# A hybrid decoder layer: head factors brought to the channels by a transpose, a small store and a broadcast load

## The chip, the cores and the metric

The kernel runs on one core of a Trainium2 chip. A core has a matrix engine (PE), a vector engine (DVE), an activation engine (ACT), a general engine (POOL) and an engine that issues transfers (SP); each works through its own queue in order, and they wait for each other on semaphores. The metric is the time of one execution on the device in microseconds (us), lower is better. Whole executions are timed several times; one more is run under the profiler, and its trace is what the readings below come from.

## The reference

One layer over 1024 tokens of 1024 channels, all in float32. Three branches read one projection of the normalized input. The parts that the change touches, cut to what matters:

```python
# RWKV-7 branch, 8 heads of 64 channels
kk = split_heads(k * k_k, 8, 64)
kk = kk / jnp.maximum(jnp.sqrt(jnp.sum(kk * kk, -1, keepdims=True)), 1e-12)
a = jax.nn.sigmoid(a0 + al @ a2)
# recurrence per token, with b = kk * a:
#   S = S * w + (S @ -kk) b^T + v k^T ;  y = S r
# stick-breaking attention, 8 heads of 64; cross attention, 4 heads of 128
k = rms_norm(split_heads(k, heads, hd), k_g)
```

In each of the three the channels of a key are divided by one number per token and head: the root of the sum of squares over the head's channels. Those numbers are the head factors.

## The kernel before

Data lies with channels on the 128 partitions and 1024 tokens along the free axis, so one tile holds two heads of 64 channels (or one of 128). A sum over channels is a sum over partitions, done on PE: `head_ss` (L267) takes 128 tokens of the squares at a time as the stationary operand and multiplies them by the two columns of `ind`, so the sums come out with tokens on partitions, 16 columns (8 groups of tokens by 2 heads). The power −0.5 runs on POOL on that small tile. To multiply the channels by the factors they must lie along the free axis again and on all channels of a head. Before the change, `expand_heads` (L249) copies each factor to 64 columns on DVE, a 128 x 1024 tile `ex`, and `bcast_heads` (L258) transposes it on PE in eight pieces of 128x128 into two PSUM banks. The product with the channels then reads PSUM.

This is done in nine places:

- `rwkv_prep` (L302), four times (p = 0 to 3), about 58 us apart from 55 us on: Sigmoids after low-rank products (L315, L316), a square of k (L320), a scan on DVE (L327), `head_ss` (L330), the power (L334), a second low-rank product (L338), exponentials (L340 to L343), `ex` (L344), transposes of v, and then the product (L366) and `b` (L367). `chain` (L376 to L379) builds operands from them on DVE, `gram` multiplies them on PE and masks the result on DVE (L393), `turned` transposes `bp` (L405).
- `sb_qk` (L746), four times, from 300 to 550 us: `k_fin` copies and squares a projection, `k_ss` makes `ex`, `k_bc` (L766) multiplies, `k_split` (L775 to L778) splits the keys for two-pass matmuls.
- `mem_kss` and `mem_kbc` (L965, L984), once, near 680 us, for the 256 memory tokens and 4 heads of 128.

How the work is ordered: functions are generators. Projections are items of eight steps; a step is six matmuls (`mm3`: two halves of three products of high and low parts). `stream` runs the items in a list, and `weave` runs one step of them for each `yield` of a main function (`rwkv_prep`, then the attention). A hook, given to an item as `{k: function}`, is called after step k. `need(name)` runs items until a named result exists. In most of the kernel the matmuls and transposes (L112, L105) are pinned: PE executes them in the order in which the program writes them. The other engines' orders are not pinned. A planner lays them out when the program is built, by its own costs and by priority (`rwkv_prep` has a higher one than the items), and each engine then keeps that order. Each weight tile is loaded by SP (L76) into one of two buffers, copied in its high part by ACT (L80), and split by POOL (L81), which frees the buffer.

Tiles come from pools with a fixed number of buffers per tag: `w4` has 3, `qk` 8, `it` 1, the PSUM tags `mm` and `g` 4 banks each.

Of the kernel before, what the change touches and what calls it, by code (L numbers as in the profile page):

```python
# [26 lines left out]
SBD = 64  # L27
# [22 lines left out]
class Trunk:  # L50
# [67 lines left out]
    def setup(self):  # L118
        nc, tc = self.nc, self.tc
        E = self.ctx.enter_context  # L120
        self.pool_c = E(tc.tile_pool(name="const", bufs=1))
        self.bufs_p = {"mm": 4, "g": 4}
        self.pool_ps = E(tc.tile_pool(name="psum", bufs=4, space=bass.MemoryType.PSUM))
        self.pool_d = E(tc.tile_pool(name="dram", bufs=1, space=bass.MemoryType.DRAM))
        self.pool_wt = E(tc.tile_pool(name="weights", bufs=2))
        self.pool_s = E(tc.tile_pool(name="small", bufs=2))
        self.kon = self.pool_c.tile([128, NKON], F32, name="kon")
        self.params = self.pool_c.tile([128, NPAR], F32, name="params")
        nc.sync.dma_start(self.params, self.I["params"])

        def kon(n):
            o, w = KON[n]
            return self.kon[:, o : o + w]

        self.ident, self.blk, self.ones = kon("ident"), kon("blk"), kon("ones")
        self.mm_mask, self.ind = kon("mm"), kon("ind")
        self.scr = self.pool_d.tile([4, NG, 128, 1024], F32, name="scr")
        self.mad = self.pool_d.tile([128, 64, 64], F32, name="mad")
        self.vd = self.pool_d.tile([2, 2, NG, 64, 4, 64], F32, name="vd")
        self.td = self.pool_d.tile([2, NG, 2, 64, 2, 128], F32, name="td")  # L140
        self.yd = self.pool_d.tile([3, 4, 128, 1024], F32, name="yd")
        self.mrd = self.pool_d.tile([8, 128, 1024], F32, name="mrd")
        self.gsd = self.pool_d.tile([3, 8, 128, 1024], F32, name="gsd")
        self.x2d = self.pool_d.tile([8, 128, 1024], F32, name="x2d")
        self.vmd = self.pool_d.tile([128, 1024], F32, name="vmd")
        self.vsd = self.pool_d.tile([T + 1, 512], F32, name="vsd")
        self.actd = self.pool_d.tile([NF // 2, 7, 128, 512], F32, name="actd")
        self.ggd = self.pool_d.tile([4, 2, 128, 1024], F32, name="ggd")

    def consts(self):  # L150
        nc = self.nc
# [94 lines left out]
        nc.vector.scalar_tensor_tensor(out, pr, self.omm[:, ti : ti + 1], tmp, ALU.mult, ALU.add)  # L246
        return out

    def expand_heads(self, f, tag="w4"):  # L249
        nc = self.nc  # L250
        ex = self.t4(tag)
        nc.vector.tensor_copy(
            ex[:, :1024].rearrange("p (j h i) -> p j h i", j=8, h=2),
            f.rearrange("p (j h) -> p j h", j=8).unsqueeze(3).to_broadcast([128, 8, 2, 64]),
        )
        return ex

    def bcast_heads(self, ex):  # L258
        out = []
# [42 lines left out]
    def rwkv_prep(self, p, krv, need):  # L302
        nc = self.nc
        lora, wa = self.lora, self.wa
        cs = slice(p * 128, (p + 1) * 128)
        halves = [slice(0, 512), slice(512, 1024)]
# [2 lines left out]
                yield  # L309
        need(f"k{p}")  # L310
        k = krv[0]
        a, su = self.t4("qk"), self.t4("qk")
        for hs in halves:
            pa, pu = self.ps("g"), self.ps("g")
            self.mmul(pa, lora[64:128, cs], wa[64:128, hs], start=True, stop=True)  # L315
            self.mmul(pu, lora[0:64, cs], wa[0:64, hs], start=True, stop=True)  # L316
            nc.scalar.activation(a[:, hs], pa, AF.Sigmoid, bias=self.par("a0", p))
            nc.scalar.activation(su[:, hs], pu, AF.Sigmoid, bias=self.par("w0", p))
        P = self.t4("qk")
        nc.scalar.activation(P, k, AF.Square, scale=self.par("k_k", p))  # L320
        kp = self.t4("qk")
        nc.scalar.activation(kp, a, AF.Identity, scale=self.par("k_a", p), bias=self.omka[:, p : p + 1])
        nc.vector.tensor_tensor(kp, k, kp, ALU.mult)
# [1 line left out]
            yield  # L325
        cc = Q = su
        nc.vector.tensor_tensor_scan(cc, self.seg, su, 0.0, ALU.mult, ALU.add)  # L327
        for _ in range(2):
            yield
        pst = self.head_ss(P)  # L330
        mx = self.small("rs", [128, 16])
        nc.vector.tensor_scalar(mx, pst, 1e-24, None, ALU.max)
        inv = self.small("inv", [128, 16])
        nc.gpsimd.tensor_tensor(inv, mx, self.half[:, :16], ALU.pow)  # L334
        g = self.t4("qk")
        for hs in halves:
            pgh = self.ps("g")
# [3 lines left out]
        pc = self.pc[p]  # L341
        nc.scalar.activation(pc, cc.rearrange("p (c s) -> p c s", c=NC)[:, :, 63], AF.Exp, scale=-EXPM)
        nc.scalar.activation(Q, cc, AF.Exp, scale=EXPM, bias=self.offs[:, 1:2])  # L343
        ex = self.expand_heads(inv, "it")  # L344
        for _ in range(3):
            yield
        need(f"v{p}")
        r, v = krv[1], krv[2]
# [13 lines left out]
        for _ in range(2):  # L362
            yield
        kk, b = k, a
        for hs, bc in zip(halves, self.bcast_heads(ex)):
            nc.vector.scalar_tensor_tensor(kk[:, hs], k[:, hs], self.par("k_k", p), bc, ALU.mult, ALU.mult)  # L366
        nc.vector.tensor_tensor(b, kk, a, ALU.mult)  # L367

        def chain(h):
            hs = halves[h]  # L370
# [298 lines left out]
                self.mmul(pt[e * 64 : e * 64 + 64, u * 4 : u * 4 + 4], vl8[0:8, u * 64 : u * 64 + 64], self.ident[0:8, e:8:2], start=True, stop=True)  # L669
        nc.vector.tensor_copy(self.vlast, pt[:, :32])  # L670

    def head_norm(self, pst, nh, width, fold, neg=None):
        nc = self.nc
        n = 8 * nh
        t = self.small("hn", [128, 16])
        v3 = lambda x: x[:, :n].rearrange("p (j h) -> p j h", j=8)
        b3 = lambda x: x.unsqueeze(2).to_broadcast([128, 8, nh])
        nc.vector.tensor_tensor(v3(t), v3(pst), b3(self.rsc2), ALU.mult)
        f = self.small("hf", [128, 16], bufs=4)
        self.rsqrt(f[:, :n], t[:, :n], n, 1.0 / (width * fold * fold), 1e-6 / (fold * fold))  # L680
        if neg is not None:
            nc.gpsimd.tensor_tensor(v3(neg), v3(f), b3(self.rscn), ALU.mult)
            return neg
        nc.gpsimd.tensor_tensor(v3(f), v3(f), b3(self.rsc), ALU.mult)
        return f

    def proj_item(self, src, fin, hook={}):
# [58 lines left out]
    def sb_qk(self, p, out):  # L746
        nc = self.nc
# [8 lines left out]
            st["k"] = sq, kr  # L756

        def k_ss():
            st["ex"] = self.expand_heads(self.head_norm(self.head_ss(st["k"][0]), 2, SBD, 1.0))

        def k_bc():
            kr = st["k"][1]
            bc = self.bcast_heads(st["ex"])
            for h in range(2):
                hs = slice(h * 512, (h + 1) * 512)
                nc.vector.scalar_tensor_tensor(kr[:, hs], kr[:, hs], self.par("sbk"), bc[h], ALU.mult, ALU.mult)  # L766
            st["K"] = [], []

        def k_split(i):
# [31 lines left out]

        w = self.I["w_in"]
        hooks = {1: lambda: k_split(1), 3: q_ss, 4: lambda: q_split(0), 6: lambda: q_split(1)}
        kq = {4: k_bc, 5: lambda: k_split(0)}
        return self.proj_item(w[18 + p], k_fin), k_ss, self.proj_item(w[14 + p], q_fin, kq), hooks

    def sb_attn(self, qk, need):
# [157 lines left out]
    def mem_kss(self):  # L965
        nc = self.nc
        sq, kr, rm, rm2 = self.mk
        pst = self.ps("g")
        for h in range(4):
            for j in range(2):  # L970
                i = h * 2 + j
                self.colsum(pst[:, i : i + 1], sq[:, i * 128 : (i + 1) * 128], self.ones[:, 0:1])
        fk = self.small("hf", [128, 16], bufs=4)
        f3 = fk[:, :8].rearrange("p (h j) -> p h j", j=2)
        b3 = lambda x: x.unsqueeze(1).to_broadcast([128, 4, 2])
        t = self.small("hn", [128, 16])
        nc.vector.tensor_tensor(t[:, :8].rearrange("p (h j) -> p h j", j=2), pst[:, :8].rearrange("p (h j) -> p h j", j=2), b3(rm2), ALU.mult)
        self.rsqrt(fk[:, :8], t[:, :8], 8, 1.0 / 128, 1e-6)
        nc.vector.tensor_tensor(f3, f3, b3(rm), ALU.mult)
        ex = self.t4()  # L980
        nc.vector.tensor_copy(ex[:, :1024].rearrange("p (i c) -> p i c", i=8), fk[:, :8].unsqueeze(2).to_broadcast([128, 8, 128]))
        self.mk = kr, ex

    def mem_kbc(self):  # L984
        nc = self.nc
        kr, ex = self.mk
        for i in range(2):
            hs = slice(i * 512, (i + 1) * 512)
            pt = self.ps("g")
            for j in range(4):  # L990
                self.transpose(pt[:, j * 128 : (j + 1) * 128], ex[:, (i * 4 + j) * 128 : (i * 4 + j + 1) * 128])
            nc.vector.tensor_tensor(kr[:, hs], kr[:, hs], pt, ALU.mult)
        self.vm = self.t4("A")
        nc.sync.dma_start(self.vm, self.vmd)
        self.kx = [self.t4("A", F32R), self.t4("A", F32R)]
        nc.scalar.activation(self.kx[0], kr, AF.Copy)
        nc.vector.tensor_tensor(self.kx[1], kr, self.kx[0].bitcast(F32), ALU.subtract)
# [691 lines left out]
    def run(self):  # L1689
# [34 lines left out]
        for h in range(4):  # L1724
            mqi[h] = self.mem_q(h, mq[h], {2: mqi[h - 1][1], 4: mark(f"mq{h - 1}")} if h > 1 else {})
        items += [gate({0: prep}), gate(), gate({2: prep}), mss, *mv, *mk, mqi[0][0], mark("kv")]
        items += [self.mem_kss, gate({1: mqi[0][1]}), self.mem_kbc, mqi[1][0], mark("mq0")]
        items += [mqi[2][0], mqi[3][0], gate({2: mqi[3][1], 4: mark("mq3")}), gate(), mark("mem")]
        ld1, br1 = self.branch(1, True)
        ld2, br2 = self.branch(2, False)  # L1730
# [113 lines left out]
```

## Time and profile before

| | |
|---|---|
| median of 3 runs | 1872.44 us (1870.16 to 1873.26) |
| the profiled execution, whole | 1876.17 us |
| its span, first to last instruction | 1874.4 us |
| mean granted PE clock | 0.988 of full speed |
| ACT, POOL busy | 886.5, 783.2 us |
| moved by DMA | 261.29 MB |

Busy time of an engine is the time in which it executes; a wait is idle time of an engine that ended when another engine or a transfer was done. In a list of instructions in order of time, a row has its start, its length, engine, line, operation, what it writes and reads, how many instructions are merged in it, and in brackets the idle time ahead of it and what ended that. A row of one line's durations has minimum, median and maximum in ns. A row of transfers has the issuing queue, the count, the size of each and the median time from issue to landing.

### The profile page before, as it was taken

The page shows a single profiled execution, that of the slowest core. Times are in us where ns is not written, and L with a number is a line of the kernel's source. Part 1 is how long each engine was busy: PE and PEld are TensorE (multiplying, and loading weights), DVE is VectorE, ACT ScalarE, POOL GpSimd, SP SyncE. Part 2 cuts the span into 40 slices and gives each one's busy share as a digit, 9 for nine tenths or more (in the row PEclk, how much of TensorE's full clock was granted, in tenths as well). Part 3 has the DMA queues.
Part 4 walks back from the last instruction along what each step waited for, and adds up shares of the span by engine and source line. Part 5 has one row for each costly group of instructions (what it writes and reads, how often), then busy time and mean ns, then how long its engine had stood idle before and what let it go on. Part 6 is the DMA issues. An engine that isn't in the chain of part 4 may idle for free. (4 is left out here: it accounts for less than half of the span.)

```text
span 1874.4 us, 27394 instructions
## 1 busy us (share of the span) xinstructions
PE 1801.7 (96%) x10468; PEld 1453.9 (78%) x10468; DVE 1170.8 (62%) x1638; ACT 886.5 (47%) x1665; POOL 783.2 (42%) x448
## 2 busy tenths in 40 slices
PE   8999999999999999998999899979999999999999
PEld 6777778778787887776777688757888888878877
DVE  5657665998887323323333682476777677785586
ACT  5443343556566635534545433454444444554433
POOL 2322342322222442112233431477676767645454
PEclk9999999999999999999999999999999999999999
DMA  4255565211112441566734573222333233386475
GB/s 177 57 172 176 166 214 162 64 48 43 51 54 66 137 109 54 191 204 227 269 126 175 173 235 111 92 88 84 113 107 107 85 124 100 125 311 211 140 240 187
DMA packets 120037, 261.29 MB, mean 139 GB/s; under 512 B 28249, under 2 KB 40793, under 8 KB 119778
## 3 DMA queue, kind: packets, MB, share of 16 engines
q1 hardware_dynamic: 82434, 193.71, 32.1%
q10 hardware_dynamic: 33696, 53.23, 7.8%
q0 software_dynamic: 3776, 12.62, 2.2%
q8 instruction: 82, 1.34, 0.3%
q14 instruction: 49, 0.40, 0.1%
HBM read 178.99 MB, written 80.48 MB: 138 GB/s over the span
## 5 line engine op out<-in xcount | busy, mean ns | idle before, releaser
L81 POOL TENSOR_TENSOR wl<-wr,wh 128x1024 fp32r<-128x1024 f32 x77 | 195.9, 2545 | 507.7 <-ACT wh L80 507.7
L112 PE MATMUL mm<-xhi,wh 128*128 128x512 f32 x784 | 265.2, 419 | 9.1 <-ACT xhi L179 7.4
L112 PE MATMUL mm<-xlo,wh 128*128 128x512 f32 x784 | 246.0, 395 | 0.9 <-DVE xlo L180 0.9
L112 PE MATMUL mm<-xhi,wl 128*128 128x512 f32 x784 | 243.8, 392 | 0.0
L112 PEld LDWEIGHTS mm<-xlo,wh 128*128 128x128 f32 x784 | 149.0, 190 | 34.8 <-DVE xlo L180 1.6
L112 PEld LDWEIGHTS mm<-xhi,wl 128*128 128x128 f32 x784 | 148.3, 189 | 33.5 <-POOL wl L81 0.5
L112 PEld LDWEIGHTS mm<-xhi,wh 128*128 128x128 f32 x784 | 139.0, 192 | 39.8 <-issue 9.1
L80 ACT ACTIVATE wh<-wr 128x1024 fp32r<-128x1024 f32 x77 | 81.4, 1057 | 158.8 <-PE mm L112 86.3
L112 PE MATMUL mm<-dw,da 128*128 128x512 f32 x528 | 121.4, 390 | 1.6 <-DVE da L1584 1.4
L112 PE MATMUL mm<-BT,wh 128*128 128x512 f32 x352 | 110.4, 395 | 7.8 <-DVE u L1397 7.8
L112 PE MATMUL mm<-BT,l 128*128 128x512 f32 x504 | 117.6, 389 | 0.0
L112 PEld LDWEIGHTS mm<-dw,da 128*128 128x128 f32 x528 | 98.8, 188 | 23.6 <-DVE da L1584 2.3
L1585 POOL TENSOR_TENSOR dw<-draw,dw 128x512 fp32r<-128x512 f32 x55 | 80.5, 1471 | 85.9 <-ACT dw L1583 83.1
L831 DVE TENSOR_TENSOR_SCAN at<-at,at 128x128 f32<-128x128 f32 (+3 forms) x64 | 91.2, 1427 | 32.1 <-ACT at L825 32.0
L112 PE MATMUL mm<-B,wh 128*128 128x512 f32 x352 | 108.5, 389 | 2.1 <-ACT p L1439 2.1
L112 PEld LDWEIGHTS mm<-BT,l 128*128 128x128 f32 x504 | 94.6, 188 | 19.6
L1584 DVE TENSOR_TENSOR da<-draw,da 128x512 fp32r<-128x512 f32 x77 | 65.9, 864 | 61.4 <-ACT da L1582 60.8
L112 PE MATMUL g<-dw,da 128*128 128x512 f32 x396 | 92.4, 394 | 3.0 <-ACT dw L1583 1.9
L733 DVE TENSOR_TENSOR w<-w,rbc 128x1024 f32<-128x1024 f32 x24 | 49.2, 2048 | 68.4 <-ACT w L732 68.3
L1345 POOL TENSOR_TENSOR l<-it,l 128x1024 fp32r<-128x1024 f32 x21 | 50.8, 2420 | 97.9 <-ACT l L1344 97.9
L112 PEld LDWEIGHTS g<-dw,da 128*128 128x128 f32 x396 | 75.5, 191 | 19.5 <-ACT dw L1583 2.3
L1582 ACT ACTIVATE da<-draw 128x512 fp32r<-128x512 f32 x77 | 48.3, 628 | 85.1 <-PE mm L112 40.8
(322 smaller groups left out, 4002.4 us busy)
## 6 DMA issues: line engine op xcount, KB each, us to landing
wr<-in_w_in_dram SPq DMA_DIRECT2D x50, 512.0 KB, 3.6
draw<-actd SPq DMA_DIRECT2D x77, 256.0 KB, 3.8
at<-scr SPq DMA_DIRECT2D x32, 512.0 KB, 5.4
draw<-in_w_down_dram SPq DMA_DIRECT2D x55, 256.0 KB, 4.9
wr<-in_w_up_dram SPq DMA_DIRECT2D x22, 512.0 KB, 3.6
actd<-gall ACTq DMA_DIRECT2D x44, 256.0 KB, 3.2
rw<-in_w_up_dram SPq DMA_DIRECT2D x20, 512.0 KB, 3.8
gsd<-w ACTq DMA_DIRECT2D x18, 512.0 KB, 2.7
```

The costliest lines, as they stand in the source:

```text
L80: self.nc.scalar.activation(hi, raw, AF.Copy)
L81: self.nc.gpsimd.tensor_tensor(lo, raw, hi.bitcast(F32), ALU.subtract)
L112: self.pinned(self.nc.tensor.matmul(*a, **k))
L733: nc.vector.tensor_tensor(g, g, self.rbc, ALU.mult)
L831: self.pinned(nc.vector.tensor_tensor_scan(sn[:, :W][:, ::-1], sn[:, :W][:, ::-1], self.smask[:, 1024 - W :][:, ::-1], 1.0, ALU.mult, ALU. ...
L1345: nc.gpsimd.tensor_tensor(lo, src, hi.bitcast(F32), ALU.subtract)
L1582: self.pinned(nc.scalar.activation(A[:, 0], a, AF.Copy))
L1584: self.pinned(nc.vector.tensor_tensor(A[:, 1], a, A[:, 0].bitcast(F32), ALU.subtract))
L1585: nc.gpsimd.tensor_tensor(Wt[:, 1], w, Wt[:, 0].bitcast(F32), ALU.subtract)
```

## The change

The nine places get the factors in another way. `factors` allocates `ex`, sets its first 128 columns to zero on POOL and lets POOL or DVE write the 16 (for memory 8) factors straight into its first columns, sorted by head and then by group of tokens. `rows_out` transposes that one block of 128x128 on PE, copies 16 rows of the result back to SBUF on ACT, and stores them (8 KB) to a small DRAM tile `fd` from ACT's queue. `rows_in` loads each head's 4 KB row from there onto all partitions of the head, from SP's queue: two loads of 64 partitions, for memory one of 128. The products read `ex` in SBUF.

In `rwkv_prep` the square and `head_ss` come ahead of the first low-rank products, one step apart from each other, and the power follows at once; `rows_out` comes ahead of the second low-rank product, `rows_in` one step after it, and `b` is made in halves. The number of steps in `rwkv_prep` stays. In `sb_qk`, `rows_out` hangs on step 2 of the Q projection, `rows_in` on step 4, `k_bc` on step 6 and the first `k_split` on step 7; before, they were on steps 4 and 5. For memory `rows_out` hangs on step 3 of a gate projection and `rows_in` on step 5.

```diff
+    def factors(self, tag="w4"):
+        ex = self.t4(tag)
+        self.nc.gpsimd.memset(ex[:, 0:128], 0.0)
+        return ex, ex[:, :16].rearrange("p (h j) -> p j h", j=8)
+
+    def rows_out(self, ex, name, n=16):
+        nc = self.nc
+        pt = self.ps("g")
+        self.transpose(pt[:, :128], ex[:, :128])
+        nc.scalar.activation(ex[0:n, 128:256], pt[0:n, :128], AF.Copy)
+        nc.scalar.dma_start(self.fd[name][0:n], ex[0:n, 128:256])
+
+    def rows_in(self, ex, name, heads=2):
+        w = 128 // heads
+        for h in range(heads):
+            self.nc.sync.dma_start(
+                ex[h * w : (h + 1) * w, :1024],
+                self.fd[name][h * 8 : (h + 1) * 8].rearrange("j p -> (j p)").unsqueeze(0).to_broadcast([w, 1024]))
...
 rwkv_prep:
+        P = self.t4("qk")
+        nc.scalar.activation(P, k, AF.Square, scale=self.par("k_k", p))
+        yield
         a, su = self.t4("qk"), self.t4("qk")
+        pst = self.head_ss(P)
         for hs in halves:
...
+        ex, inv = self.factors("it")
+        mx = self.small("rs", [128, 16])
+        nc.vector.tensor_scalar(mx, pst, 1e-24, None, ALU.max)
+        nc.gpsimd.tensor_tensor(inv, mx.rearrange("p (j h) -> p j h", j=8), self.half[:, :16].rearrange("p (j h) -> p j h", j=8), ALU.pow)
...
         nc.vector.tensor_tensor_scan(cc, self.seg, su, 0.0, ALU.mult, ALU.add)
-        for _ in range(2):
-            yield
-        pst = self.head_ss(P)
...
+        yield
+        self.rows_out(ex, f"r{p}")
         g = self.t4("qk")
...
-        ex = self.expand_heads(inv, "it")
-        for _ in range(3):
+        yield
+        self.rows_in(ex, f"r{p}")
+        for _ in range(2):
             yield
...
-        for hs, bc in zip(halves, self.bcast_heads(ex)):
-            nc.vector.scalar_tensor_tensor(kk[:, hs], k[:, hs], self.par("k_k", p), bc, ALU.mult, ALU.mult)
-        nc.vector.tensor_tensor(b, kk, a, ALU.mult)
+        for hs in halves:
+            nc.vector.scalar_tensor_tensor(kk[:, hs], k[:, hs], self.par("k_k", p), ex[:, hs], ALU.mult, ALU.mult)
+            nc.vector.tensor_tensor(b[:, hs], kk[:, hs], a[:, hs], ALU.mult)
...
 sb_qk:
-            st["ex"] = self.expand_heads(self.head_norm(self.head_ss(st["k"][0]), 2, SBD, 1.0))
+            st["ex"], f = self.factors()
+            self.head_norm(self.head_ss(st["k"][0]), 2, SBD, 1.0, into=f)
...
+            nc.vector.scalar_tensor_tensor(kr, kr, self.par("sbk"), st.pop("ex"), ALU.mult, ALU.mult)
...
-        kq = {4: k_bc, 5: lambda: k_split(0)}
+        kq = {2: lambda: self.rows_out(st["ex"], f"s{p}"), 4: lambda: self.rows_in(st["ex"], f"s{p}"), 6: k_bc, 7: lambda: k_split(0)}
...
 run:
-        items += [self.mem_kss, gate({1: mqi[0][1]}), self.mem_kbc, mqi[1][0], mark("mq0")]
+        items += [self.mem_kss, gate({1: mqi[0][1], 3: lambda: self.rows_out(self.mk[1], "m", 8), 5: lambda: self.rows_in(self.mk[1], "m", 1)}), self.mem_kbc, mqi[1][0], mark("mq0")]
```

More of the change, by code (lines that the diff above doesn't have):

```diff
@@ L148, in setup @@
         self.ggd = self.pool_d.tile([4, 2, 128, 1024], F32, name="ggd")
+        self.fd = {n: self.pool_d.tile([16, 128], F32, name=f"fd{n}") for n in ("r0", "r1", "r2", "r3", "s0", "s1", "s2", "s3", "m")}
     def consts(self):
@@ L247, in shifted @@
         return out
-    def expand_heads(self, f, tag="w4"):
-        nc = self.nc
[L251 to L256, printed above, removed]
+    def factors(self, tag="w4"):
[3 more added lines that the diff above has]
+    def rows_out(self, ex, name, n=16):
+        nc = self.nc
+        pt = self.ps("g")
[8 more added lines that the diff above has]
+                self.fd[name][h * 8 : (h + 1) * 8].rearrange("j p -> (j p)").unsqueeze(0).to_broadcast([w, 1024]))
     def bcast_heads(self, ex):
@@ L318, in rwkv_prep @@
             nc.scalar.activation(su[:, hs], pu, AF.Sigmoid, bias=self.par("w0", p))
-        P = self.t4("qk")
-        nc.scalar.activation(P, k, AF.Square, scale=self.par("k_k", p))
+        ex, inv = self.factors("it")
+        mx = self.small("rs", [128, 16])
+        nc.vector.tensor_scalar(mx, pst, 1e-24, None, ALU.max)
+        nc.gpsimd.tensor_tensor(inv, mx.rearrange("p (j h) -> p j h", j=8), self.half[:, :16].rearrange("p (j h) -> p j h", j=8), ALU.pow)
         kp = self.t4("qk")
@@ L327, in rwkv_prep @@
         nc.vector.tensor_tensor_scan(cc, self.seg, su, 0.0, ALU.mult, ALU.add)
-        for _ in range(2):
-            yield
-        pst = self.head_ss(P)
[L331 to L334, printed above, removed]
+        yield
+        self.rows_out(ex, f"r{p}")
         g = self.t4("qk")
@@ L670, in spread_last, with head_norm @@
         nc.vector.tensor_copy(self.vlast, pt[:, :32])
-    def head_norm(self, pst, nh, width, fold, neg=None):
+    def head_norm(self, pst, nh, width, fold, neg=None, into=None):
         nc = self.nc
@@ L683, in head_norm @@
             return neg
-        nc.gpsimd.tensor_tensor(v3(f), v3(f), b3(self.rsc), ALU.mult)
+        nc.gpsimd.tensor_tensor(v3(f) if into is None else into, v3(f), b3(self.rsc), ALU.mult)
         return f
@@ L758, in k_ss @@
         def k_ss():
-            st["ex"] = self.expand_heads(self.head_norm(self.head_ss(st["k"][0]), 2, SBD, 1.0))
+            st["ex"], f = self.factors()
+            self.head_norm(self.head_ss(st["k"][0]), 2, SBD, 1.0, into=f)
         def k_bc():
             kr = st["k"][1]
[L763 to L766, printed above, removed]
+            nc.vector.scalar_tensor_tensor(kr, kr, self.par("sbk"), st.pop("ex"), ALU.mult, ALU.mult)
             st["K"] = [], []
@@ L978, in mem_kss @@
         self.rsqrt(fk[:, :8], t[:, :8], 8, 1.0 / 128, 1e-6)
-        nc.vector.tensor_tensor(f3, f3, b3(rm), ALU.mult)
-        ex = self.t4()
-        nc.vector.tensor_copy(ex[:, :1024].rearrange("p (i c) -> p i c", i=8), fk[:, :8].unsqueeze(2).to_broadcast([128, 8, 128]))
+        ex, _ = self.factors()
+        nc.vector.tensor_tensor(ex[:, :8].rearrange("p (h j) -> p h j", j=2), f3, b3(rm), ALU.mult)
         self.mk = kr, ex
@@ L986, in mem_kbc @@
         kr, ex = self.mk
[L987 to L992, printed above, removed]
+        nc.vector.tensor_tensor(kr, kr, ex, ALU.mult)
         self.vm = self.t4("A")
```

## The prediction

> **What bounds the kernel now.** I read the page first, then busy time by stretch, then the waits of PE in the stretch where the change acts, then single instructions in order of time.
>
> ```profile
> span 1874.4 us, 27394 instructions
> PE 1801.7 (96%) x10468; PEld 1453.9 (78%) x10468; DVE 1170.8 (62%) x1638; ACT 886.5 (47%) x1665; POOL 783.2 (42%) x448
> ...
> 39.90:300.00 260.10, 250.36 (x1386) 192.70 (x1385) 159.80 (x190) 107.69 (x131) 86.14 (x39) 0.99 0.51 161
> 300.00:700.00 400.00, 391.40 (x2681) 321.73 (x2680) 290.16 (x282) 221.81 (x398) 124.78 (x64) 1.00 0.24 72
> ...
> PE g L105 <- DVE at L393: 6.4, 3, 2.5
> PE g L112 <- DVE qk L379: 2.4, 2, 1.8
> ```
>
> The first two lines are the whole kernel, the next two the stretches that hold the four `rwkv_prep` (40 to 300) and the `sb_qk` and memory work (300 to 700): length, then busy us of PE, PEld, DVE, ACT, POOL. PE is idle 9.7 us of 260 and 8.6 us of 400. So the kernel is PE in a fixed order, and a microsecond of PE removed here is nearly a microsecond of the end, unless a wait replaces it. The last two lines are waits of PE from 45 to 300: total, times, longest. They are 8.8 us, both for DVE, and both behind the multiplication by the head factors.
>
> **Removed from PE.** Each of nine places (four preps, four `sb_qk`, one memory K) loses eight transposes and gains one.
>
> ```profile
> 82.25 0.62 PE L112 MATMUL mm<-xlo,wh 128*128 128x512 f32 x2
> 82.70 0.62 PE L112 MATMUL mm<-xhi,wl 128*128 128x512 f32 x2
> 83.16 1.03 PE L105 MATMUL g<-kon,it 128*128 128x128 f32 x8
> 84.50 0.62 PE L112 MATMUL mm<-xlo,wh 128*128 128x512 f32 x2
> ...
> 380.18 0.62 PE L112 MATMUL mm<-xhi,wl 128*128 128x512 f32 x2
> 380.64 0.27 PE L105 MATMUL g<-kon,at 128*128 128x128 f32 x1
> 381.21 0.62 PE L112 MATMUL mm<-xlo,wh 128*128 128x512 f32 x2
> ...
> L105 PE MATMUL g<-kon,it x96: 270/272/447, 83.2 to 287.1; 128*128 128x128 f32 x96
> ```
>
> A pair of matmuls starts 0.45 to 0.46 us after the one before (82.25 and 82.70; 380.18 and the transpose at 380.64); I take 0.457. From 82.70 to 84.50 lie two pairs and the eight transposes: 1.80 − 2 × 0.457 = 0.88 us. From 380.18 to 381.21 lie two pairs and one transpose: 1.03 − 0.91 = 0.12 us. Per place 0.88 − 0.12 = 0.76, nine places **−6.8 us**. That the 32 small column-sum matmuls of a prep move from beside L338 to beside L315/L316 keeps their number, and the number of groups of f32 work between the pairs: nothing.
>
> A duration of 272 ns is not that price, since the records overlap: eight of them fit in 1.03 us. The Trainium skill, page "TensorE: Matmul & The Clock Gate", section "Part 4: PE-mode transpose", gives about 275 ns for a transpose inside a kernel; by it the term would be an estimated 63 × 0.275 = 17.3 us instead of 6.8. The duration agrees with the row, the spacing doesn't, and I go by the spacing.
>
> **A wait that is added on PE.** In `sb_qk` the one transpose is issued after k = 2 of the Q projection, the eight stood after k = 4; PE's order is pinned, so everything behind it waits until POOL has written the factors.
>
> ```profile
> 310.10 1.10 PE L112 MATMUL g<-kon,w 128*64 128x2 f32 x32
> 317.61 0.61 PE L112 MATMUL mm<-xhi,wl 128*128 128x512 f32 x2
> 318.10 1.07 PE L105 MATMUL g<-kon,w 128*128 128x128 f32 x8
> 313.09 3.84 POOL L166 TENSOR_TENSOR hf<-rs,half 128x16 f32<-128x16 f32 x1 [0.80 <-DVE rs L165]
> 317.01 0.22 POOL L684 TENSOR_TENSOR hf<-hf,rsc 128x16 f32<-128x16 f32 x1
> ...
> 453.48 0.22 POOL L684 TENSOR_TENSOR hf<-hf,rsc 128x16 f32<-128x16 f32 x1
> 454.43 0.62 PE L112 MATMUL mm<-xhi,wl 128*128 128x512 f32 x2
> ```
>
> For p = 0 nothing else runs on PE in between: k = 4 ends at 317.61 + 0.46 = 318.07, one step is three pairs or 1.37 us, so k = 2 ends at 315.3. The factors are there at 317.23 (column sums from 310.1 to 311.2, 1.9 us until POOL begins, its power of 3.84, and 0.22). PE waits **+1.9** us; the old group, at 318.10, waited for nothing. For p = 2 attention work lies between: k = 2 ends at 454.89, the factors are there at 453.70, 1.2 us ahead; p = 1 and 3 look alike. Ends: 0 if the 1.9 us between the sums and POOL vanish, +5 if the other three slip 1 us past their lead. The new memset of `ex` (128x128) is the one POOL operation added ahead of the power; beside it a prep's power and the low-rank products:
>
> ```profile
> 130.07 1.98 PE L112 MATMUL g<-A,A 128*128 128x512 f32 x4
> L478 POOL MEMSET it<- x1: 515/515/515, 727.5 to 727.5; 128x512 f32 x1
> 130.45 2.93 POOL L334 TENSOR_TENSOR inv<-rs,half 128x16 f32<-128x16 f32 x1 [5.57 <-DVE rs L332]
> 145.16 1.90 POOL L405 TENSOR_TENSOR it<-qk,pc 128x1024 f32<-128x1024 f32 x1 [11.78 <-DVE qk L376]
> ```
>
> A quarter of 0.515 is 0.13 us, inside that lead. In the preps the sums now come two steps earlier and the transpose 3 steps and the low-rank products (2.0 us) behind them, about 6.1 us; the maximum on DVE, the power (2.93) and the handing over need about 3.5 (an estimate), and POOL idles 5.57 us ahead of that power: no wait. The Square that the earlier sums need has a whole step ahead of it on ACT: nothing, at the worst a microsecond (an estimate). The memory transpose stands two steps behind its factors: nothing.
>
> **The way through DRAM, and what it frees.** ACT copies 16 rows, stores 8 KB, SP loads twice 256 KB. At p = 1:
>
> ```profile
> yd<-ys ACTq DMA_DIRECT2D x16, 128.0 KB, 2.2
> wr<-in_w_in_dram SPq DMA_DIRECT2D x50, 512.0 KB, 3.6
> inst<-mad POOLq DMA_DIRECT2D x4, 512.0 KB, 7.2
> 129.77 1.13 ACT L244 ACTIVATE w<-w,params 128x1023 f32<-128x1023 f32 x1
> L252 DVE COPY it<-inv x4: 694/694/2872, 70.2 to 247.6; 128x1024 f32<-128x1024 f32 x4
> 140.90 1.41 DVE L366 SCALAR_TENSOR_TENSOR at<-at,params,g 128x512 f32<-128x512 f32 x2 [0.75 <-PE g L105]
> 124.91 25.86 SPq L76 DMA_DIRECT2D wr<-in_w_in_dram  x2
> ```
>
> Before L338's matmuls lie as many steps and the same work as now, so the transpose is at about 130.1; ACT is free at 130.9, its copy ends by 131.3. The store lands in 2.2 (nearest row, though larger), the loads in 3.6 plus 0.4 for the second issue: **137.5**, bounds 137 and 141 (by 7.2). The old product started at 140.90. It no longer waits for eight transposes on PE, and DVE loses the expanding copy (L252, 0.69 us) ahead of it, while the product in halves adds one small operation. At p = 0 the eight stood at 83.16 behind `need("v0")`, and DVE idled for them:
>
> ```profile
> 83.80 1.41 DVE L366 SCALAR_TENSOR_TENSOR at<-at,params,g 128x512 f32<-128x512 f32 x2 [3.97 <-PE g L105]
> 103.11 1.94 PE L105 MATMUL g<-kon,it 128*128 128x128 f32 x8 [2.27 <-DVE at L393]
> 152.96 1.16 PE L112 MATMUL g<-qk,qk 64*128 64x128 f32 x16 [1.76 <-DVE qk L379]
> ```
>
> With the factors landed near 75, DVE can use those 3.97 us, and the wait of 2.27 behind its backlog goes; at p = 1 a product up to 3 us earlier takes the 1.76. I credit these two, **−4.0**; ends 0 and −8.8 (all waits of both lines). What is late next is the other 4.8 us of the same two lines, at p = 2 and 3, which I leave. In `sb_qk` the product moves from k = 4 to k = 6 and DVE may stand for a landing:
>
> ```profile
> 460.73 1.41 DVE L766 SCALAR_TENSOR_TENSOR w<-w,params,g 128x512 f32<-128x512 f32 x2 [0.94 <-PE g L105]
> 462.06 0.95 DVE L831 TENSOR_TENSOR_SCAN at<-at,at 128x384 f32<-128x384 f32 x1
> 468.81 0.49 PE L105 MATMUL g<-kon,at 128*128 128x128 f32 x3
> ```
>
> At p = 2: transpose at 454.9, ACT 0.5 to 1 (an estimate), store 2.2, loads 4.0: landed near 462, a good 1 us after the old product's start, and up to 2 us of DVE standing still. Queued behind it on DVE is the scan of 462.06; who needs that are three transposes at 468.81, 5.8 us after its end. Nothing on PE; without that cover 2 us a place. The nine ACT copies and stores stand on an engine that is busy 47%: nothing.
>
> Sum on the profiled execution (1876.2 us, of which 1.8 lie outside the span): −6.8 + 1.9 − 4.0 = **−8.9**, so 1867.3. That execution stands 3.7 above the median of the runs, 1872.4, which gives **1863.5**. No change, here, is within 0.2% (3.7 us).
>
> **The rivals.**
>
> *SP's order parks the load (slower).* SP works in order, and stands for 681 us on weight loads that wait for POOL to free their buffer.
>
> ```profile
> SPq L76 <- POOL wl L81: 681.3, 67, 25.1
> ```
>
> Total, times, longest. At p = 1 the second load of the row of 124.91 leaves at 150.4. If the broadcast is queued behind it instead of ahead of it, it lands at 154.4 where 140.9 was needed: 13.5 us later, on the gram matmuls that already wait for that chain at 152.96. The sum is then −8.9 + 1.8 + 13.5 = +6.4, 1878.8. It decides once the factors land after about 148, where 7 us of lateness eat the gain. Against it: the queue's order follows the planned times, and the broadcast is due 13 us ahead of that load. For it: at p = 2 and 3 and in attention the margins are smaller (a few us), and planned landings are not measured ones.
>
> *Products that meet POOL.* The new products read two operands from SBUF, the old ones one from PSUM.
>
> ```profile
> L350 DVE SCALAR_TENSOR_TENSOR qk<-at,params,qk x4: 1276/1280/2956, 70.8 to 241.8; 128x1024 f32<-128x1024 f32 x4
> ```
>
> Such an operation took 1.28 us, and 2.96 once, beside a weight split: 1.7 lost. On the gram path of all four preps that is +6.7 and the sum −2.2, 1870.2: same. Against it: at p = 1 POOL idles 11.78 us up to 145.16. The Trainium skill, page "SBUF — State Buffer", section "SBUF: two separate sides", says why: a DVE operation with two SBUF inputs and a GpSimd one share a port pair as an exclusive lock. The 2.96 agrees.
>
> *Transposes worth their duration.* 63 × 0.272 = 17.1, so −17.1 + 1.9 − 4.0 = −19.2, 1853.2. The spacing speaks against it.
>
> **How the numbers follow.** Forecast 0.62 (own range 1856.8 to 1867.5: the credit from −8.8 to 0, the wait at p = 0 from 0 to 1.9), long transposes 0.03, same 0.15 (the port, or several waits of 1 to 2 us), parked load 0.20. The range of all runs from −15.6 (all 8.8 credited, no wait at p = 0), 1856.8, to the parked load's 1878.8. Faster 0.65, same 0.15, slower 0.20.
>
> **What would show it.** Right: nine groups of one transpose instead of eight, PE busy in 40 to 700 down by some 7 us or more by the records; one PE wait of about 2 us for POOL near 315 and none at the other three; the 2.27 and 1.76 gone; broadcast loads landing within 4 us, issued ahead of the weight load of their time. Wrong: DVE waiting over 5 us for a load of `ex`, PE waits for POOL at each single transpose, or PE idle in 40 to 700 above today's 18 us by as much as its work fell.

## The result and the profile after

Slower: 1892.3 us median of 4 runs (1888.08 to 1902.61), against 1872.85 (1870.16 to 1876.88) for the kernel before on the same chip, a ratio of 1.011 (95% interval 1.0065 to 1.0156). Forecast were 1863.5 and a range of 1856.8 to 1878.8. The execution in the profile is the slowest of the four (1902.61); its totals carry that, its single readings do not.

The page of the kernel after, the two stretches in which the change acts (length, busy us of PE, PEld, DVE, ACT, POOL, granted clock), and the waits of PE there (from 45 to 300, then from 300 to 700):

```profile
span 1900.8 us, 27363 instructions
PE 1818.6 (96%) x10405; PEld 1452.6 (76%) x10405; DVE 1165.1 (61%) x1628; ACT 888.6 (47%) x1674; POOL 787.6 (41%) x457
...
40.00:300.00 260.00, 248.63 (x1345) 189.12 (x1344) 154.44 (x190) 107.00 (x131) 88.47 (x41) 0.98 0.54 169
300.00:700.00 400.00, 387.52 (x2613) 315.23 (x2612) 281.98 (x266) 219.79 (x399) 123.60 (x67) 0.99 0.25 76
...
PE g L105 <- DVE at L406: 5.6, 2, 3.1
PE g L105 <- DVE at L247: 2.8, 1, 2.8
PE g L112 <- ACT qk L324: 2.0, 1, 2.0
...
PE g L112 <- ACT w L795: 2.0, 1, 2.0
...
PE g L105 <- POOL w L697: 0.3, 1, 0.3
```

PE has 63 instructions fewer, as forecast, and yet is busy 16.9 us longer over the whole. The list of waits grew by 5.5 us (18.3 to 23.8 from 45 to 700), so most of the loss is no wait: the instructions that are left take longer. Which ones, the groups by line and tile say (busy us, mean ns of one), first of the kernel before (in `mm<-x,w` the moving operand, which streams through, stands first and the stationary one, the weights, second):

```profile
L112 PE MATMUL mm<-xhi,wl 128*128 128x512 f32 x784 | 243.8, 392 | 0.0
L112 PE MATMUL mm<-B,l 128*128 128x512 f32 x264 | 63.6, 390 | 1.6 <-DVE u L1461 1.6
L112 PE MATMUL mm<-dw,da 128*128 128x512 f32 x528 | 121.4, 390 | 1.6 <-DVE da L1584 1.4
```

and of the kernel after:

```profile
L112 PE MATMUL mm<-xhi,wl 128*128 128x512 f32 x784 | 249.3, 400 | 1.1 <-POOL wl L81 1.1
L112 PE MATMUL mm<-B,l 128*128 128x512 f32 x264 | 65.3, 396 | 1.6 <-DVE u L1466 1.6
L112 PE MATMUL mm<-dw,da 128*128 128x512 f32 x528 | 121.6, 390 | 2.2 <-DVE da L1589 2.0
```

The change touches none of these lines. Two of the three groups are slower in a kernel that issues them unchanged, one is not. A stretch far behind the change, with no wait in it, gives the spacing; twelve matmuls of one accumulation and the row behind them, before and after:

```profile
1402.48 2.88 PE L112 MATMUL mm<-B,l 128*128 128x512 f32 x12
1405.20 0.62 PE L112 MATMUL mm<-B,wh 128*128 128x512 f32 x2
```

```profile
1406.91 2.96 PE L112 MATMUL mm<-B,l 128*128 128x512 f32 x12
1409.71 0.62 PE L112 MATMUL mm<-B,wh 128*128 128x512 f32 x2
```

2.72 us for twelve before, 2.80 after: 227 ns and 233 ns from one matmul to the next. Over all pairs of neighbouring matmuls that are 220 to 246 ns apart, the sum of what lies above 226.7 ns is 6.7 us before and 23.7 us after. The difference, 17.0 us, is most of the loss of 19 us between the medians.

**What changed for them is the address.** In the kernel before the power of a prep writes a small tile of its own, `inv = self.small("inv", [128, 16])`: two buffers of 64 bytes on each partition. The change writes the power into `ex` and the tile is gone. Tiles are laid out one behind the other, so 45 of the 90 tile names, all that lie behind `inv` on its side of the memory, moved down by 128 bytes: in the compiled program the first `xhi` lies at 45952 instead of 46080, and all `xhi`, `xlo` and `l` and some of the tiles behind `B` and `BT` moved likewise. `wh`, `wl`, `dw` and `da` stayed. 46080 is a multiple of 256, 45952 isn't.

Set beside these addresses, the trace of the kernel after says more than that. Where only the moving operand had moved (`xhi`, `xlo` and part of `B`, with `wh` or `wl`), the matmuls are 232.4 ns apart in the mean; where only the weights had (`B,l` above), 233.0. `BT,l` has both cases: `l` moved, and so did one half of `BT`, while the other half stayed. The two halves follow each other, eleven matmuls of each:

```profile
1393.14 2.66 PE L112 MATMUL mm<-BT,l 128*128 128x512 f32 x11
1396.10 2.72 PE L112 MATMUL mm<-BT,l 128*128 128x512 f32 x11
```

One record lasts 0.39, so ten steps take 2.27 and 2.33 us. In the first row both operands lie 128 bytes off a multiple of 256, and it is not slower: all 252 such pairs are 226.8 ns apart, the 252 of the second kind 232.6. What costs, then, is not an odd address by itself but that the two operands of a matmul no longer lie a multiple of 256 bytes apart. The rule isn't exact: sixteen more pairs with both operands moved, which stand two at a time among slow ones (`mm<-wo_sp,mg`), are 231.4 ns apart.

### The profile page after: what moved, and what is told of

The parts are those of the page before. It is cut to its first block, busy times and chain, and to the rows that moved or that the text cites. A ratio compares the mean times of both kernels' runs of the same rounds, so it can differ in the third digit from the quotient of the medians.

```text
span 1900.8 us, 27363 instructions
## 1 busy us (share of the span) xinstructions
PE 1818.6 (96%) x10405; PEld 1452.6 (76%) x10405; DVE 1165.1 (61%) x1628; ACT 888.6 (47%) x1674; POOL 787.6 (41%) x457
## 5 line engine op out<-in xcount | busy, mean ns | idle before, releaser
L112 PE MATMUL mm<-xhi,wh 128*128 128x512 f32 x784 | 269.0, 424 | 10.2 <-ACT xhi L180 7.5
L112 PE MATMUL mm<-xlo,wh 128*128 128x512 f32 x784 | 250.5, 401 | 0.7 <-DVE xlo L181 0.7
L112 PE MATMUL mm<-xhi,wl 128*128 128x512 f32 x784 | 249.3, 400 | 1.1 <-POOL wl L81 1.1
L746 DVE TENSOR_TENSOR w<-w,rbc 128x1024 f32<-128x1024 f32 x24 | 53.3, 2220 | 61.7 <-ACT w L745 61.5
```

The costliest lines, as they stand in the source:

```text
L112: self.pinned(self.nc.tensor.matmul(*a, **k))
L746: nc.vector.tensor_tensor(g, g, self.rbc, ALU.mult)
```

## The experiments

Each was timed in five rounds with the kernel before on the same chip.

**The address alone.** First the changed kernel with an unused buffer, so that all matmul operands lie where they lay before:

```diff
+        self.pool_s.tile([128, 32], F32, name="pad", tag="pad", bufs=1)
```

> The changed kernel with one unused buffer of 128 bytes per partition, so that every tile stands at the address it has in the kernel before (the change drops the small tile inv, which moved xhi, xlo and all later tiles of that side down by 128 bytes); no instruction differs. Theory A, the address: the matmuls that were 232 ns apart go back to 227 to 228, about 17 us come back, and the time falls from 1892 to 1875, plus or minus 5; what stays against the kernel before, 0 to 9 us, is the change itself. Theory B, a state of the chip in those executions: the spacing and the time stay as they are for the change, or both kernels move together, 1892. Theory C, the new waits and the half-clock stretches behind them cost it all: 1888 to 1893.

1875.34 us beside 1875.66, ratio 1.0003 (0.9991 to 1.0016). Not one instruction differs from the changed kernel. The stretch from above in this kernel:

```profile
1400.83 2.88 PE L112 MATMUL mm<-B,l 128*128 128x512 f32 x12
1403.55 0.62 PE L112 MATMUL mm<-B,wh 128*128 128x512 f32 x2
```

2.72 again. The other way round, the kernel before with the same tiles moved down by 128 bytes, by giving `inv` to the group of another small tile:

```diff
-        inv = self.small("inv", [128, 16])
+        inv = self.small("hf", [128, 16], bufs=4)
```

> The kernel before, with inv put into the small tiles that hf uses, so that the same later tiles stand 128 bytes lower, as in the changed kernel; every engine executes the same instructions in the same order. Theory A: matmuls with a moved operand are about 232 ns apart, the time rises by some 17 us to 1889, plus or minus 4. Theory B and C: no change, 1872, plus or minus 3.

1887.77 us, ratio 1.0065 (1.005 to 1.0079). The kernel before with 256 unused bytes (`[128, 64]` in the line of the first diff):

> The kernel before with one unused buffer of 256 bytes, so that the same tiles stand 256 bytes higher. Theory A does not say which alignment counts: if 256 bytes are enough, 1872; if 512 or 1024 are needed, 1885 to 1892. Theory B and C: 1872.

1873.69 us, 0.9993 (0.9981 to 1.0004). And the changed kernel once more, beside these:

> The changed kernel once more, unchanged, for a second profile beside the others on one chip. Theory A: 1888 to 1894 and matmuls 232 ns apart again, in the same tiles. Theory B: the spacing is another one this time, and the time follows it.

1890.06 us, 1.0078 (1.0063 to 1.0092). Two more, later, in the kernel before: 64 unused bytes, and 128 unused bytes without any joined buffers.

> The kernel before with an unused buffer of 64 bytes per partition ahead of the small tiles; no instruction differs, 45 of the 90 tile names move up by 64 bytes (the weight-product operand xhi0 from 46080 to 46144). Theory A (a matmul pays where its operands' addresses are no multiples of 256 bytes): the pairs are about 232 ns apart instead of 227.5 and the time is 1885 to 1891, as with 128 bytes. Rival B (only an odd multiple of 128 bytes pays): 1873, and pairs 227.5 ns apart.

> The kernel before with an unused buffer of 128 bytes per partition ahead of the small tiles; nothing else differs from before (the earlier move of these tiles down by 128 bytes also joined two small tiles into one group of buffers). Theory A: 1885 to 1891, the loss of the changed kernel without any part of the change. Rival: 1873, and the earlier loss came from the joined buffers.

1882.32 us, 1.0046 (1.0034 to 1.0058), and 1887.36 us, 1.0078 (1.0063 to 1.0092). The twelve matmuls with 64 bytes, then with 128:

```profile
1403.09 2.96 PE L112 MATMUL mm<-B,l 128*128 128x512 f32 x12
1405.89 0.63 PE L112 MATMUL mm<-B,wh 128*128 128x512 f32 x2
```

```profile
1403.59 2.96 PE L112 MATMUL mm<-B,l 128*128 128x512 f32 x12
1406.38 0.62 PE L112 MATMUL mm<-B,wh 128*128 128x512 f32 x2
```

233 ns in both. So a kernel with no edit but 128 unused bytes loses what the changed kernel lost beside it (13.7 and 14.4 us by the medians), and the changed kernel with 128 unused bytes loses nothing. That is shown. The 17 us of the spacing are not reached: with 128 unused bytes the mean granted clock was higher than beside it (0.9887 and 0.9868, worth 3.4 us), but for the moved `inv` (12.1 us) and the changed kernel again (14.4) the clocks agree, and 3 to 5 us stay open. Both theories on 64 bytes missed the total: the `B` matmuls pay in full, but `xhi,wl` stands at 229.0 ns there and at 232.8 with 128 bytes, and the sum over all pairs is 18.9 us instead of 24.0. The split from above holds in both: with both operands moved `BT,l` stays at 227.0 and 227.1 ns, with the weights alone it is at 233.3 and 232.6. Why a moving operand that moved alone pays less at 64 (230.1 ns in the mean) stays open, and so does why the distance counts at all.

**What the rest of the change does, at equal addresses.** From here on all kernels have the addresses of the kernel before. The padded kernel made no measurable difference where −8.9 us was forecast. Its waits of PE are nearly those of the changed kernel, and two places at p = 0 show what happened. First the prep, in the kernel after, all engines in order of need:

```profile
59.17 1.15 ACT L324 ACTIVATE qk<-at,params 128x1024 f32<-128x1024 f32 x1 [1.35 <-DVE at L247]
60.37 1.10 PE L112 MATMUL g<-kon,qk 128*64 128x2 f32 x32 [2.03 <-ACT qk L324]
67.61 0.27 PE L105 MATMUL g<-kon,it 128*128 128x128 f32 x1
70.24 0.25 ACT L259 ACTIVATE it<-g 16x128 f32<-16x128 f32 x1
71.96 1.14 SPq L265 DMA_DIRECT2D it<-fdr  x2
77.80 1.41 DVE L379 SCALAR_TENSOR_TENSOR at<-at,params,it 128x512 f32<-128x512 f32 x2 [2.48 <-DMA it<-fdr]
78.75 2.73 POOL L81 TENSOR_TENSOR wl<-wr,wh 128x1024 fp32r<-128x1024 f32 x1 [7.40 <-ACT wh L80]
79.13 3.49 DVE L380 TENSOR_TENSOR qk<-at,qk 128x512 f32<-128x512 f32 x2
144.89 1.29 DVE L380 TENSOR_TENSOR qk<-at,qk 128x512 f32<-128x512 f32 x2
86.38 1.35 PE L105 MATMUL g<-kon,at 128*128 128x128 f32 x8 [2.79 <-DVE at L247]
```

The key of p = 0 is ready only shortly before the square, so the sums, now the first thing in the prep, wait 2.03 us for it. The single transpose needs nothing, but its result is copied 2.6 us later, because the copy stands in ACT's queue behind an exponential; the factors land at 77.8, 10.2 us behind the transpose. DVE stands 2.48 us for them, and the second product then runs beside a weight split on POOL and takes 3.49 us, where the same two instructions took 1.29 at p = 1 (144.89). What is queued behind them on DVE is the mix that makes v (L247), and PE waits 2.79 us to transpose it. Then the first `sb_qk`, in the padded kernel:

```profile
309.97 1.10 PE L112 MATMUL g<-kon,w 128*64 128x2 f32 x32
312.71 1.06 PE L112 MATMUL mm<-xhi,wh 128*128 128x512 f32 x2
313.57 1.06 PE L112 MATMUL mm<-xlo,wh 128*128 128x512 f32 x2
317.34 0.33 PE L105 MATMUL g<-kon,w 128*128 128x128 f32 x1 [0.34 <-POOL w L698]
325.29 3.50 DVE L778 SCALAR_TENSOR_TENSOR w<-w,params,w 128x1024 f32<-128x1024 f32 x1 [6.63 <-ACT wh L80]
390.60 1.28 DVE L778 SCALAR_TENSOR_TENSOR w<-w,params,w 128x1024 f32<-128x1024 f32 x1
...
332.09 1.39 PE L112 MATMUL g<-kon,w 128*64 128x2 f32 x32 [2.12 <-ACT w L796]
334.43 1.05 PE L112 MATMUL mm<-xlo,wh 128*128 128x512 f32 x2
335.28 1.05 PE L112 MATMUL mm<-xhi,wl 128*128 128x512 f32 x2
```

DVE stands 6.63 us ahead of the product and the product takes 3.50 us instead of 1.28 (390.60, the second place). The releaser named, ACT's `wh`, is none of the product's operands; a kernel below shows the load in its place. What ACT does behind the product comes late, and PE waits 2.12 us for the square of q (L796). Rows 312.71 and 334.43 show a second thing: pairs that are 0.85 us apart instead of 0.46. PE ran at half its clock there, 3.4 us at a time.

Three kernels move the two waits. One puts the sums of the first prep one step behind its low-rank products and the transpose right behind the scan; one moves the first `k_split` to step 0 of the item that follows; one does both:

```diff
-        pst = self.head_ss(P)
+        if p:
+            pst = self.head_ss(P)
...
+        if p == 0:
+            yield
+            pst = self.head_ss(P)
...
-        yield
+        if p:
+            yield
         self.rows_out(ex, f"r{p}")
```

> The padded change (tiles at the addresses of before). In the first prep alone the column sums come one step behind the first low-rank products instead of ahead of them, and the single transpose comes right after the scan. Theory A (the change's gain is real and is given back by waits at p = 0): PE's 2.3 us for the Square and its 2.9 us at v's transposes with the half-clock stretch behind it (1.7) shrink, 3 to 6 us less than the padded change, 1869 to 1872. Theory C (the gain isn't there, whatever waits): the same as the padded change, 1875.

```diff
-        hooks = {1: lambda: k_split(1), 3: q_ss, 4: lambda: q_split(0), 6: lambda: q_split(1)}
-        kq = {2: lambda: self.rows_out(st["ex"], f"s{p}"), 4: lambda: self.rows_in(st["ex"], f"s{p}"), 6: k_bc, 7: lambda: k_split(0)}
+        hooks = {0: lambda: k_split(0), 1: lambda: k_split(1), 3: q_ss, 4: lambda: q_split(0), 6: lambda: q_split(1)}
+        kq = {2: lambda: self.rows_out(st["ex"], f"s{p}"), 4: lambda: self.rows_in(st["ex"], f"s{p}"), 6: k_bc}
```

> The padded change, with the first k_split moved from step 7 of the Q projection to step 0 of the gate projection after it, so that ACT's Square of q does not stand behind copies that wait for the product. Theory A: PE's wait of 2.1 us for that Square near 332 and the half-clock stretch there (6.8 us at half speed, 3.4 lost) go, 3 to 5 us less than the padded change, 1870 to 1872. Theory C: 1875.

> Both edits together. Theory A: the two gains add, 6 to 11 us less than the padded change, 1864 to 1869. Theory C: 1875.

1874.83 us (0.9998, 0.9988 to 1.0009), 1876.61 (1.0006, 0.9994 to 1.0018) and 1875.6 (1.0003, 0.9991 to 1.0015), each beside 1875.6: nothing, as theory C had it. The waits moved and did not go. With both edits PE's waits are

```profile
PE g L105 <- POOL it L342: 3.5, 1, 3.5
...
PE g L112 <- DVE qk L811: 2.5, 1, 2.5
```

the transpose of the prep now for POOL, whose power comes later, and the first attention matmuls for the split that was put off. DVE's row shows what stood behind the 6.63:

```profile
321.95 1.28 DVE L783 SCALAR_TENSOR_TENSOR w<-w,params,w 128x1024 f32<-128x1024 f32 x1 [6.53 <-DMA w<-fds]
```

It is the broadcast load. At the first `sb_qk` no other work is there to cover it.

**The change at fewer places.** The old functions were kept beside the new ones and used at p = 0, so that seven of the nine places have the change:

```diff
-            kp, kss, qp, hooks = self.sb_qk(p, qk[p])
+            kp, kss, qp, hooks = (self.sb_qk if p else self.sb_qk_old)(p, qk[p])
...
-            self.weave(self.rwkv_prep(p, krv[p], need), pump, 1.0)
+            self.weave((self.rwkv_prep if p else self.rwkv_prep_old)(p, krv[p], need), pump, 1.0)
```

> The change at seven of the nine places only: the first prep and the first sb_qk are as in the kernel before; tiles at the addresses of before. Theory A: seven times 0.76 us of PE, 5.3, and the waits and half-clock stretch of the second prep, which went in the padded change (about 3), so 1866 to 1870 where the kernel before has 1874 to 1875. Theory C: 1873 to 1875.

1872.78 us, 0.9989 (0.9975 to 1.0003): by its ratio better than the padded change by some 2 to 3 us, its distance from the kernel before not clear of nothing, and the time lies between the ranges of the two theories. In the memory place DVE stands longest of all for its load, here in the kernel after:

```profile
DVE w L997 <- DMA w<-fdm: 10.6, 1, 10.6
```

so the next kernel does the memory K the old way too.

> The change at six of its nine places, the preps and sb_qk of p = 1 to 3; the first prep, the first sb_qk and the memory K the old way; addresses as before. Theory A (the p = 0 places have no work to cover the way through DRAM; in the memory K, DVE stands about 10 us for its load, which costs 1 to 2 us of PE between 610 and 670): 1869 to 1872, ratio 0.998. Rival B (the memory place costs nothing, the 1 to 2 us there are the half-clock stretches falling otherwise): 1872.5 to 1874, 0.9995.

1871.4 us beside 1873.66, 0.9989 (0.998 to 0.9998). This is the one version that beats both kernels, by about 2 us, with an upper end that just clears 1; as one of several versions tried, that is weak evidence. The time lies in theory A's range, the ratio between the two theories. That the memory place costs anything is not shown: both kernels have the same ratio.

**What the removed transposes are worth by themselves.** The kernel before, with one transpose instead of eight and products that read its block four times over; no store, no load, no copy. It leaves out seven eighths of the factors and only measures time.

```diff
-        out = []
-        for h in range(2):
-            pt = self.ps("g")
-            for j in range(4):
-                self.transpose(pt[:, j * 128 : (j + 1) * 128], ex[:, (h * 4 + j) * 128 : (h * 4 + j + 1) * 128])
-            out.append(pt)
-        return out
+        pt = self.ps("g")
+        self.transpose(pt[:, :128], ex[:, :128])
+        return [pt[:, :128].unsqueeze(1).to_broadcast([128, 4, 128])] * 2
```

> The kernel before, addresses as before; at each of the nine places one 128x128 transpose instead of eight, and the products read this one block of PSUM four times over: it leaves out seven eighths of the head factors, adds no store, no load, no copy and no memset, and moves nothing. It measures what the removed PE work alone can bring. Theory A (the term of the prediction, 0.76 us a place, is real and the way through DRAM gave it back in new waits): 1866 to 1869, ratio 0.9965. Rival B (PE's spacing makes up for it later, or the waits behind DVE grow by what PE is earlier): 1871 to 1874, ratio within 0.001 of 1.

The edit also reaches a tenth place, the norm factors at the start (L234), so ten groups shrink. 1874.78 us, 1.0003 (0.9992 to 1.0014): nothing, as rival B had it. PE's waits in the preps, and the stretches 175 to 228 and 300 to 345 (length, PE, PEld, DVE, ACT, POOL, granted clock), in this kernel:

```profile
PE g L105 <- DVE at L392: 12.3, 4, 3.4
...
175.00:228.00 53.00, 49.58 (x267) 37.82 (x267) 32.96 (x42) 22.68 (x28) 16.63 (x8) 0.94 0.47 146
300.00:345.00 45.00, 45.00 (x276) 37.03 (x275) 33.70 (x45) 19.14 (x22) 16.59 (x8) 0.96 0.28 85
```

and the same stretches of the kernel before:

```profile
175.00:228.00 53.00, 50.71 (x299) 38.56 (x298) 36.29 (x45) 21.66 (x27) 16.40 (x8) 1.00 0.47 148
300.00:345.00 45.00, 43.45 (x279) 35.70 (x278) 36.14 (x47) 19.36 (x24) 17.60 (x8) 1.00 0.24 77
```

At nine of the ten places the two pairs around a group take 0.77 us less (mostly 1.80 before, 1.03 now), so the price of a group was right. But the waits for the masked product of `gram` and for `chain`, 8.8 us before, are 12.3: in the preps DVE, not PE, sets the pace, and PE's earliness becomes a longer wait. What takes up the rest, in `sb_qk` and behind it, is not shown. In these two profiles the clock also differs, 0.94 and 0.96 where it was 1.00 (53 × 0.06 = 3.2 and 45 × 0.04 = 1.8 us), but that is not this edit's: in the four profiles of the kernel before with other addresses the second stretch has 0.96 twice and the first 0.97 once, and over all runs the mean clock costs this kernel 1.1 us.

A balance, in us: what PE lost in work at 0.76 a group, the sum of its list of waits from 45 to 700 (18.3 before), and the mean granted clock over all runs, as time (0.001 is 1.87 us):

| kernel | PE work | waits | clock | sum | measured (medians) |
|---|---|---|---|---|---|
| padded change, nine places | −6.8 | 23.6, +5.3 | +1.7 | +0.2 | −0.3 |
| one transpose, ten places | −7.6 | 22.5, +4.2 | +1.1 | −2.3 | +1.1 |
| change at seven places | −5.3 | 18.3, 0 | −0.9 | −6.2 | −2.8 |
| change at six places | −4.6 | 20.2, +1.9 | −1.2 | −3.9 | −2.3 |

The sums have the order of the measured values except for the second row, and lie up to 3.4 us too low. The waits are those of one profile each, and two profiles of one kernel differ by as much (the changed kernel: 23.8 and 20.8); what happens behind 700 is not in them. So the balance shows the size of the terms and decides nothing between the rows, and these few us stay open.

## Why the prediction was wrong

**The step that failed** is the first one: that PE's spacing is a constant, 0.457 us for a pair, and only the instructions removed and the waits added count. The sum had no term for the tile that the change deletes. Its removal moved one operand of most of the 512-column matmuls by 128 bytes against the other and cost 17 us by the spacing, twice what the whole forecast was about. No rival had it either; the range's upper end, 1878.8, was the price of another mechanism, and the result lies above it. In the diff the line that did it, `inv` without a tile of its own, stood in plain sight, and the row that would have priced it did not exist in the trace of before.

**At equal addresses** the sum still missed: −8.9 forecast, no difference measured. Term by term:

- *PE work, −6.8.* The price of a group was right (0.77 at nine places). That a microsecond off PE is a microsecond off the end was wrong: without the way through DRAM it brought nothing, in the preps because the waits for DVE grew by 3.5 us.
- *The wait of 1.9 for POOL at the first `sb_qk`.* 0.3 in the profiles of the changed and the padded kernel. PE came later to the transpose, because it ran at half its clock in between (rows 312.71 and 313.57); the time was lost another way. In the second profile of the changed kernel the clock fell only behind the transpose, and the wait was there in full, so the term was right:

```profile
319.19 0.33 PE L105 MATMUL g<-kon,w 128*128 128x128 f32 x1 [1.92 <-POOL w L697]
```

- *The credit of 4.0.* The waits of 2.27 and 1.76 went, as forecast (8.8 us on those lines became 5.6). In their place came waits that the sum had at nothing: the square ("at the worst a microsecond", measured 2.0), v behind DVE's stop at p = 0 (2.8), the square of q behind the late product (2.0). In the second profile of the changed kernel the last two are missing, and PE lost 3.4 us to half clock at p = 0 and the 1.92 above instead. That the two waits went was in part luck: PE itself was later (the transposes of v at p = 1 began at 138.99 in the padded kernel, 136.55 before), and the product at p = 1 came at 142.42, not up to 3 us ahead of 140.90.
- *Landing at p = 0 "near 75".* 77.8. The copy on ACT, costed at nothing since ACT is busy 47%, came 2.6 us after its transpose. Transpose to product took 10.2 us there; the transfers themselves were as estimated:

```profile
it<-fdr SPq DMA_DIRECT2D x8, 256.0 KB, 4.0
w<-fds SPq DMA_DIRECT2D x8, 256.0 KB, 3.9
```

- *SP's order (rival, 0.20).* It did not happen; the loads left 1.4 us behind the store's issue (row 71.96), and 3.7 us at the latest (p = 3), with no weight load in between.
- *Products that meet POOL (rival, 0.15).* It happened at two places of nine, 3.49 and 3.50 us instead of 1.28. The size was 2.2 us each, not 1.7. The outcome it gave, "same", is what the padded kernel shows, but not by four such products in the preps: one was there, the other in `sb_qk`. The Trainium skill, page "SBUF — State Buffer", section "SBUF: two separate sides", has the reason: DVE with two SBUF inputs and GpSimd lock each other out. The rows agree: the split ran from 78.75 to 81.48 and the product from 79.13 to 82.62.
- *Transposes at their full duration (rival, 0.03).* Excluded: in the kernel with one transpose a group gives back 0.77 us and not 7 × 0.272 = 1.9, and the end gains nothing.

## What to carry to other kernels

An edit that adds or drops even a small tile moves all tiles behind it: compare the addresses of the matmul operands before and after, keep the two operands of a matmul a multiple of 256 bytes apart (most simply both at multiples of 256, as in the kernel before), and time an edit against a control with unused bytes in place of the tile. A matmul group that shows the same count and no wait but a longer mean is the sign to look for. And a microsecond taken off the busiest engine is worth a microsecond only where no other engine is at its heels; a wait that stands just behind the removed work is the first thing to read.

## What the hardware showed that was not expected

- Matmuls of 128x512 in f32 of which one operand had been moved by 128 bytes against the other followed each other in 232 to 233 ns, otherwise in 227 (`mm<-B,l`: 2.80 and 2.72 us for twelve); by 64 bytes it was 228 to 233, depending on the group. A move by 256 bytes cost nothing, and neither did a move of both operands by 64 or 128 (`mm<-BT,l`, 227 ns). Legal addresses, then, are not equally fast.
- The granted clock falls to half for 3.4 us, or a multiple, in the middle of the kernel, and each 3.4 us cost about 1.7 us. In each profile all such stretches start a multiple of 3.41 us apart, so they fall elsewhere in another execution: the changed kernel has one from 315.77 in one profile and from 319.49 in the other. They come behind PE waits of about 2 us (334.43 behind a wait of 2.12) and also without any wait (from 315.86 in the kernel with one transpose, where 64 small matmuls, column sums among them, fill 313.54 to 315.60). The Trainium skill, page "TensorE: Matmul & The Clock Gate", section "Part 1: The HAM clock gate (the "warmup" mystery)", lets the clock fall after an idle window of about 3.4 us; the length of 3.4 us agrees, the idle time needed ahead of it does not: the longest wait of PE in the first `sb_qk` was 2.12 us.
